# Row-run query tiles, fewer loads, accumulating dots and an event-listed end phase in a hard-max attention kernel

## The chip, the cores and the metric

The kernel runs on one core of one Trainium2 chip. The metric is the device time of one execution in microseconds (us), median over the runs.

## The reference

Four batches of 4096 queries and 4096 keys, 128 elements each, fp32. For each query the value row of the key with the largest dot product is wanted, nothing else.

```
def reference(q, k, v):                                   # each 4 x 4096 x 128, fp32
    logits = np.matmul(q, k.transpose(0, 2, 1))
    best = np.argmax(logits, axis=-1)
    b_idx = np.arange(q.shape[0])[:, None]
    return v[b_idx, best, :].astype(np.float32)
```

## The kernel before

The 128 query tiles (T = 128, 128 queries each) go through a pipeline of five engines, one tile per step of a loop that emits all engines' work in a fixed order:

- PE (TensorE) makes fp16 scores, folded so that one column stands for a group of four keys.
- ACT (ScalarE) evicts them: twice an absolute value (`A<-pd`) and once a relu (`E<-psn`).
- DVE (VectorE) takes the maximum over two halves (`W<-psn,E`, here "the fold") and then the eight largest (`TOP<-W`).
- POOL (GpSimd) gathers for each query the fp16 key differences of its best group (`kg`); DVE makes three dot products with the query (`D`) and picks the key, in chunks of 8 tiles; POOL gathers the value rows (`vr`); SP stores them.
- Near ties are found by `flag_segment` (twice: tiles 0-63, tiles 64-127) and solved again in fp32: gathers FR, FQ, three FK, exact dots, gather FV, scatter into the output.

POOL's work waits in three lists: `near_q` holds the key gathers, `fast` the gathers and the scatter of the re-check, `late_q` the value gathers and the stores. The *issue rule* says how many of each go out in one step.

The parts that the argument touches, with cuts marked:

```
def load_q(b, x, y):                     # a tile is 128 successive rows: runs of 512 bytes
    nc.gpsimd.dma_start(out=natq[b % 2][:, x:y], in_=q[b].rearrange("(t p) d -> p t d", p=P)[:, x:y])

def dots(c, x, m):                       # for m = 2 tiles
    yield "until", lambda: ("kg", x) in done, 2
    ...                                  # prod = kg * q;  p1, p2: two halving adds
    nc.vector.tensor_reduce(out=d[:, x - c0:x - c0 + m, 1:4], in_=p2, axis=AX_X, op=OP.add)

def issue(it):                           # once a step: what POOL is given
    if it > T + 1:
        while near_q:
            near_q.pop(0)()
        late = 2
    else:
        n = 0
        while near_q and (n < 1 or near_q[0] in marks):        # one key gather
            g = near_q.pop(0)
            n += g not in marks
            g()
        late = 2 if n == 0 and len(late_q) + len(fast) > 4 else 1   # and one value gather
    for _ in range(late):
        if fast or late_q:
            (late_q if late_q and it > T + 1 else fast or late_q).pop(0)()
        ...
```

Of the kernel before, what the change touches and what calls it, by code (L numbers as in the profile page):

```python
# [7 lines left out]
FP32 = mybir.dt.float32  # L8
# [13 lines left out]
TAU = 8.0  # L22
NEAR = 0.5


@with_exitstack
def kernel(ctx, tc, q, k, v, out):
# [24 lines left out]
    rec = dr.tile([P * T, 8], U32, name="rec")  # L52
    k16 = [dr.tile([NG, 384], FP16, name=f"k16_{b}") for b in range(B)]
# [5 lines left out]

    def load_k(b, h, x, y):  # L60
        kb = k[b].rearrange("(h p n) d -> p h n d", p=P, n=16)
        nc.gpsimd.dma_start(out=natk[b % 2][:, h, x:y], in_=kb[:, h, x:y])  # L62

    def load_q(b, x, y):
        nc.gpsimd.dma_start(out=natq[b % 2][:, x:y], in_=q[b].rearrange("(t p) d -> p t d", p=P)[:, x:y])  # L65
# [10 lines left out]
    def load_part(b, i):  # L76
        if b >= B:
            return
        if i < 8:
            load_k(b, i // 4, i % 4 * 4, i % 4 * 4 + 4)  # L80
        else:
            load_q(b, (i - 8) * NQT // 8, (i - 7) * NQT // 8)
# [18 lines left out]
    nc.vector.tensor_scalar(out=identn, in0=ident, scalar1=-1.0, scalar2=None, op0=OP.mult)  # L101
    for h in range(2):
        put_k(0, h)
    D_t = [cp.tile([P, 8, 4], FP32, name=f"D{i}", tag=f"D{i}") for i in range(3)]
# [23 lines left out]
    nc.gpsimd.tensor_scalar(out=tri, in0=iota_r, scalar1=iota_p, scalar2=1.0, op0=OP.subtract, op1=OP.is_gt)  # L128
    HARD = cp.tile([P, 1], FP32, tag="HARD")
# [100 lines left out]
    done, stores, marks = set(), set(), set()  # L230

    def gather(c, t0, n):
        c0, c1 = chunks[c]
        if t0 == c0:
            cand_t[c] = sp.tile([P, c1 - c0], U32, tag=f"cand{c1 - c0}", name=f"cand_{c}", bufs=3)
        x = cand_t[c][:, t0 - c0:t0 - c0 + n]
        nc.vector.tensor_scalar(out=x, in0=TOP.bitcast(U32)[:, t0:t0 + n, 0], scalar1=NG - 1, scalar2=NG - 1,
                                op0=OP.bitwise_and, op1=OP.bitwise_xor)
        kg = rp.tile([P, n, 3, P], FP16, tag=f"kg{n}", name=f"kg_{t0}", bufs=8)
        assert len(kg_t) < 8  # L240
        kg_t[t0] = kg
        for j in range(n):
            near_q.append(lambda j=j: nc.gpsimd.indirect_dma_start(  # L243
                out=kg[:, j].rearrange("p f d -> p (f d)"), out_offset=None, in_=k16[t0 // NQT],
                in_offset=IOA(ap=x[:, j:j + 1], axis=0)))
        mark = lambda: done.add(("kg", t0))
        marks.add(mark)
        near_q.append(mark)
        start(dots(c, t0, n), "dots")

    def dots(c, x, m):
        c0 = chunks[c][0]
        d = D_t[c % 3]
        b = x // NQT
        yield "until", lambda: ("kg", x) in done, 2
        kg = kg_t.pop(x)
        prod = rp.tile([P, m, 3, P], FP16, tag=f"prod{m}", name=f"prod_{x}")
        nc.vector.tensor_tensor(out=prod, in0=kg, in1=natq[b % 2][:, x - b * NQT:x - b * NQT + m, :].unsqueeze(2).to_broadcast([P, m, 3, P]),  # L258
                                op=OP.mult)
        yield "dve",  # L260
        p1 = rp.tile([P, m, 3, 64], FP16, tag=f"p1{m}", name=f"p1_{x}")
        nc.vector.tensor_tensor(out=p1, in0=prod[:, :, :, 0:64], in1=prod[:, :, :, 64:128], op=OP.add)  # L262
        yield "dve",
        p2 = rp.tile([P, m, 3, 32], FP16, tag=f"p2{m}", name=f"p2_{x}")
        nc.vector.tensor_tensor(out=p2, in0=p1[:, :, :, 0:32], in1=p1[:, :, :, 32:64], op=OP.add)  # L265
        yield "dve",
        nc.vector.tensor_reduce(out=d[:, x - c0:x - c0 + m, 1:4], in_=p2, axis=AX_X, op=OP.add)  # L267
        done.add(("dot", x))

    def pick(c, t0, t1):  # L270
        n = t1 - t0
        b, qt = t0 // NQT, t0 % NQT
        d = D_t[c % 3][:, 0:n, :]
        yield "until", lambda: all(("dot", x) in done for x in range(t0, t1, 2)), 0
# [3 lines left out]
        yield "dve",  # L278
        lt = sp.tile([P, n, 4], FP32, tag=f"lt{n}", name=f"lt_{c}")
        nc.vector.tensor_tensor(out=lt, in0=d, in1=mx.to_broadcast([P, n, 4]), op=OP.is_lt)  # L280
        yield "dve",
# [3 lines left out]
        yield "dve",  # L285
        wi = sp.tile([P, n], FP32, tag=f"wi{n}", name=f"wi_{c}")
        nc.vector.tensor_reduce(out=wi, in_=sel, axis=AX_X, op=OP.min)
        yield "dve",
        win = sp.tile([P, n], U32, tag=f"win{n}", name=f"win_{c}")
        nc.vector.scalar_tensor_tensor(out=win, in0=cand, scalar=4.0, in1=wi, op0=OP.mult, op1=OP.add)  # L290
        vr = rp.tile([P, n, P], FP32, tag=f"vr{n}", name=f"vr_{c}", bufs=3)
        for j in range(n):
            late_q.append(lambda j=j: nc.gpsimd.indirect_dma_start(out=vr[:, j, :], out_offset=None, in_=v_flat,  # L293
                                                                   in_offset=IOA(ap=win[:, j:j + 1], axis=0)))

        def store():
            nc.sync.dma_start(out=out[b, qt * P:(qt + n) * P, :].rearrange("(j p) d -> p j d", p=P), in_=vr)
            done.add(("out", c))

        stores.add(store)  # L300
        late_q.append(store)
        yield "dve",
# [3 lines left out]
        yield "dve",  # L306
        nc.vector.tensor_reduce(out=CNT[:, t0:t1], in_=near, axis=AX_X, op=OP.add)
        done.add(("cnt", c))

    def put_rec(t0, t1):  # L310
        nc.sync.dma_start(out=rec.rearrange("(p t) w -> p t w", t=T)[:, t0:t1, :], in_=TOP.bitcast(U32)[:, t0:t1, :])



    def flag_segment(t0, t1, ready, stored):
        yield "until", ready, 0
        S = t1 - t0
        H = fp.tile([P, S, 4], U32, tag="H", name=f"H_{t0}")
        nc.vector.tensor_scalar(out=H, in0=TOP.bitcast(U32)[:, t0:t1, 0:4], scalar1=16, scalar2=None,
                                op0=OP.logical_shift_right)  # L320
        yield "dve", 0.17
        F = fp.tile([P, S], FP32, tag="F", name=f"F_{t0}")
        nc.vector.scalar_tensor_tensor(out=F, in0=H[:, :, 1], scalar=TAU, in1=H[:, :, 0], op0=OP.add, op1=OP.is_ge)
        yield "dve", 0.17
        nc.vector.scalar_tensor_tensor(out=F, in0=CNT[:, t0:t1], scalar=1.5, in1=F, op0=OP.is_gt, op1=OP.max)
        yield "dve", 0.17
        F4 = fp.tile([P, S], FP32, tag="F4", name=f"F4_{t0}")
        nc.vector.scalar_tensor_tensor(out=F4, in0=H[:, :, 3], scalar=TAU, in1=H[:, :, 0], op0=OP.add, op1=OP.is_ge)
        yield "dve", 0.17
        Ec = fp.tile([P, S], FP32, tag="Ec", name=f"Ec_{t0}")  # L330
        nc.vector.tensor_tensor(out=Ec, in0=F, in1=codes[:, t0:t1], op=OP.mult)
        yield "dve", 0.17
        e8 = fp.tile([P, 8], FP32, tag="e8", name=f"e8_{t0}")
        nc.vector.max(out=e8, in_=Ec)
        yield "dve", 0.17
        val = fp.tile([P, 8], FP32, tag="val", name=f"val_{t0}")
        nc.vector.tensor_scalar(out=val, in0=e8, scalar1=0.5, scalar2=None, op0=OP.is_gt)
        yield "dve", 0.17
        n2 = fp.tile([P, 3], FP32, tag="n2", name=f"n2_{t0}")
        nc.vector.tensor_reduce(out=n2[:, 0:1], in_=val, axis=AX_X, op=OP.add)  # L340
        yield "dve", 0.17
        nc.vector.tensor_reduce(out=n2[:, 1:2], in_=F, axis=AX_X, op=OP.add)
        yield "dve", 0.17
        nc.vector.tensor_reduce(out=n2[:, 2:3], in_=F4, axis=AX_X, op=OP.add)
        yield "dve", 0.17
        yield "wait", 2
        ps = pp.tile([P, 1024], FP32, tag="u", name=f"fp_{t0}")
        nc.tensor.matmul(out=ps[:, 0:1], lhsT=tri, rhs=n2[:, 0:1], start=True, stop=True)  # L348
        nc.tensor.matmul(out=ps[:, 512:515], lhsT=ones, rhs=n2, start=True, stop=True)
        bs = fp.tile([P, 1], FP32, tag="bs", name=f"bs_{t0}")  # L350
        nc.vector.tensor_copy(out=bs, in_=ps[:, 0:1])
        yield "dve", 0.17
        tot = fp.tile([P, 3], FP32, tag="tot", name=f"tot_{t0}")
        nc.vector.tensor_copy(out=tot, in_=ps[:, 512:515])
        yield "dve", 0.17
        posn = fp.tile([P, 8], FP16, tag="posn", name=f"posn_{t0}")
        nc.vector.scalar_tensor_tensor(out=posn, in0=iota_r[:, 0:8], scalar=bs, in1=val, op0=OP.add, op1=OP.mult)
        yield "dve", 0.17
# [3 lines left out]
        yield "dve", 0.17  # L362
        rec2 = fp.tile([P, 8, 2], BF16, tag="rec2", name=f"rec2_{t0}")
        nc.vector.tensor_copy(out=rec2[:, :, 0], in_=e8)
        yield "dve", 0.17
        nc.vector.tensor_copy(out=rec2[:, :, 1], in_=iota_p.to_broadcast([P, 8]))
        yield "dve", 0.17
        yield "wait", 2
        ps2 = pp.tile([P, 1024], FP32, tag="u", name=f"fq_{t0}")
        for s in range(8):  # L370
            nc.tensor.matmul(out=ps2[:, 0:2], lhsT=OH[:, s, :], rhs=rec2[:, s, :], start=s == 0, stop=s == 7)
        tp = fp.tile([P, 2], FP32, tag="tp", name=f"tp_{t0}")
        nc.vector.tensor_copy(out=tp, in_=ps2[:, 0:2])
        yield "dve", 0.17
        rw = fp.tile([P, 2], FP32, tag="rw", name=f"rw_{t0}")
        nc.vector.tensor_scalar(out=rw[:, 0:1], in0=tp[:, 0:1], scalar1=0.5, scalar2=float(1 << 20), op0=OP.is_lt, op1=OP.mult)
        yield "dve", 0.17
        nc.vector.scalar_tensor_tensor(out=rw[:, 1:2], in0=tp[:, 0:1], scalar=float(P), in1=tp[:, 1:2], op0=OP.mult, op1=OP.add)
        yield "dve", 0.17
        row = fp.tile([P, 1], U32, tag="row", name=f"row_{t0}")  # L380
        nc.vector.scalar_tensor_tensor(out=row, in0=rw[:, 1:2], scalar=-float(P), in1=rw[:, 0:1], op0=OP.add, op1=OP.add)
        yield "dve", 0.17

        hd = fp.tile([P, 2], FP32, tag="hd", name=f"hd_{t0}")
        nc.vector.tensor_scalar(out=hd[:, 0:1], in0=tot[:, 1:2], scalar1=-float(P), scalar2=0.0, op0=OP.add, op1=OP.max)
        yield "dve", 0.17
        nc.vector.tensor_tensor(out=hd[:, 1:2], in0=tot[:, 1:2], in1=tot[:, 0:1], op=OP.subtract)
        yield "dve", 0.17
        for a in (hd[:, 0:1], hd[:, 1:2], tot[:, 2:3]):
            nc.vector.tensor_tensor(out=HARD, in0=HARD, in1=a, op=OP.add)  # L390
            yield "dve", 0.17

        rr = fp.tile([P, 1], U32, tag="rr", name=f"rr_{t0}")
        nc.vector.scalar_tensor_tensor(out=rr, in0=tp[:, 1:2], scalar=float(T), in1=tp[:, 0:1], op0=OP.mult, op1=OP.add)
        yield "dve", 0.17
# [20 lines left out]
        for r in range(3):  # L416
            get(FK[:, r, :], k4, gb[:, r:r + 1], B * NG)
# [215 lines left out]
```

## Time and profile before

| what | value | from |
|---|---|---|
| time | 502.46 us (501.86 to 503.29) | three runs |
| span | 498.3 us | the page; this execution took 500.26 us |
| first fold, last fold start | 20.8, 429.6 us | timeline of DVE |
| last fold to span end ("end phase") | 68.7 us | the same |
| per tile, tiles 20 to 75 | 3.15 us | fold start to fold start |

From the page, the busy time of each engine, and the busy tenths of DVE and ACT and the granted PE clock in 40 slices of the span:

```profile
PE 399.9 (80%) x1960; PEld 187.9 (38%) x1960; DVE 420.5 (84%) x833; ACT 394.5 (79%) x441; POOL 310.7 (62%) x345
...
DVE  2179999999999999999999899999999999972030
ACT  1999999999999999999989899999878999200000
...
PEclk9999999999999999999999999999999999755555
```

Two engines are full until the last fold. The windows say where each one binds (columns: stretch, its length, busy us of PE, PEld, DVE, ACT, POOL with instruction counts, granted clock, DMA share, GB/s): ACT in 75-100, where the next batch is transposed, and DVE in 200-250.

```profile
75.00:100.00 25.00, 23.13 (x125) 10.78 (x124) 23.80 (x41) 25.00 (x32) 15.23 (x16) 1.00 0.33 62
200.00:250.00 50.00, 47.20 (x212) 20.42 (x211) 50.00 (x91) 48.11 (x53) 34.84 (x39) 1.00 0.38 90
```

The waits of three groups (busy us, mean ns, then the engine's idle time just before them and what ended it). The closing re-check waits 20.0 us for its first gather, FR, which stands behind a backlog of value gathers on POOL:

```profile
L223 DVE TENSOR_TENSOR W<-psn,E 128x1024 int16<-128x1024 f32 x128 | 166.5, 1301 | 25.5 <-ACT E L210 16.4
L188 PEld LDWEIGHTS <-qT 128*128 128x128 f16 x1024 | 99.7, 99 | 159.3 <-issue 71.6
L411 DVE TENSOR_SCALAR gi<-FR 128x3 uint32<-128x3 uint32 x2 | 0.3, 157 | 20.0 <-DMA FR<-rec,rr 20.0
```

### The profile page before, as it was taken

The numbers are of one execution on the slowest core, as the hardware profiler recorded it, in microseconds if no ns is written. First come the engines' busy times: TensorE is split into PE (matmuls) and PEld (weight loads), VectorE is DVE, ScalarE is ACT, GpSimd is POOL, SyncE is SP. The second block draws the span as 40 slices with busy tenths as digits, with TensorE's granted clock in tenths as the row PEclk, the third lists the DMA queues.
The fourth block names the chain that finished last, engine by engine and source line by source line (L and its number), as shares of the span: only waits on it lengthen the run. The fifth ranks groups of instructions, "written<-read, shape, count | busy, mean of one in ns | idle before, by whom it ended". The sixth has DMA issues, their size and how long they took to land. (4 is left out here: it accounts for less than half of the span.)

```text
span 498.3 us, 6462 instructions
## 1 busy us (share of the span) xinstructions
PE 399.9 (80%) x1960; PEld 187.9 (38%) x1960; DVE 420.5 (84%) x833; ACT 394.5 (79%) x441; POOL 310.7 (62%) x345
## 2 busy tenths in 40 slices
PE   8999999999899999999999899989988999200000
PEld 5545554444345544443455444333333333100000
DVE  2179999999999999999999899999999999972030
ACT  1999999999999999999989899999878999200000
POOL 9124446566787886667888866566646666677730
PEclk9999999999999999999999999999999999755555
DMA  9714354132547672315456641323311313243410
GB/s 131 134 17 81 81 94 74 54 98 55 124 94 157 114 128 65 99 53 113 96 130 136 88 98 55 91 57 93 98 39 54 98 54 97 57 123 95 110 52 5
DMA packets 51751, 43.47 MB, mean 87 GB/s; under 512 B 24424, under 2 KB 45931, under 8 KB 51712
## 3 DMA queue, kind: packets, MB, share of 16 engines
q0 software_dynamic: 31520, 30.97, 31.3%
q1 hardware_dynamic: 20192, 12.06, 8.3%
q8 instruction: 15, 0.25, 0.2%
q14 instruction: 24, 0.20, 0.1%
HBM read 39.59 MB, written 12.19 MB: 104 GB/s over the span
## 5 line engine op out<-in xcount | busy, mean ns | idle before, releaser
L197 ACT ACTIVATE A<-pd 128x1024 f16<-128x1024 f32 x256 | 267.9, 1083 | 8.8 <-PE pd L188 8.4
L243 POOL DMA_INDIRECT kg<-k,cand x128 | 124.1, 970 | 123.3 <-DVE p L262 30.7
L223 DVE TENSOR_TENSOR W<-psn,E 128x1024 int16<-128x1024 f32 x128 | 166.5, 1301 | 25.5 <-ACT E L210 16.4
L188 PE MATMUL psn<-kT,qT 128*128 128x512 f16 x512 | 151.8, 377 | 19.5 <-ACT A L197 13.0
L188 PEld LDWEIGHTS <-qT 128*128 128x128 f16 x1024 | 99.7, 99 | 159.3 <-issue 71.6
L188 PE MATMUL pd<-kT,qT 128*128 128x512 f16 x512 | 152.4, 379 | 6.5 <-ACT A L197 6.2
L226 DVE MAX8 TOP<-W 128x8 f32<-128x1024 f32 x128 | 155.9, 1218 | 0.0
L207 PE MATMUL psn<-A,identh 128*128 128x512 f16 x512 | 152.0, 378 | 0.0
L293 POOL DMA_INDIRECT vr<-in_v_dram,win x128 | 126.9, 992 | 39.0 <-issue 36.9
L210 ACT ACTIVATE E<-psn 128x1024 int16<-128x1024 f32 x128 | 138.0, 1078 | 7.8 <-PE psn L207 7.1
L207 PEld LDWEIGHTS <-identh 128*128 128x128 f16 x512 | 49.5, 97 | 60.8
L258 DVE TENSOR_TENSOR prod<-kg,natq 128x768 f16<-128x768 f16 (+1 forms) x65 | 35.1, 541 | 2.9 <-DMA kg<-k,cand 2.9
L262 DVE TENSOR_TENSOR p<-prod 128x384 f16<-128x384 f16 (+1 forms) x65 | 22.3, 346 | 0.0
L65 POOL DMA_DIRECT2D natq<-in_q_dram x26 | 22.3, 858 | 0.1
L160 PE MATMUL uk<-identh,natk 128*128 128x128 f16 x96 | 22.2, 303 | 0.0
L267 DVE TENSOR_REDUCE D<-p 128x6 f32<-128x192 f16 (+1 forms) x65 | 21.6, 333 | 0.0
L163 ACT ACTIVATE kT<-uk 128x512 f16<-128x512 f32 x24 | 14.6, 606 | 4.2 <-PE uk L161 3.5
L170 ACT ACTIVATE qT<-uq 128x512 f16<-128x512 f32 x24 | 17.1, 710 | 0.9 <-PE uq L168 0.9
L411 DVE TENSOR_SCALAR gi<-FR 128x3 uint32<-128x3 uint32 x2 | 0.3, 157 | 20.0 <-DMA FR<-rec,rr 20.0
L348 PE MATMUL fp<-n,tri 128*128 128x1 f32 x4 | 0.9, 304 | 20.1 <-DVE n L340 20.1
L62 POOL DMA_DIRECT2D natk<-in_k_dram x26 | 15.7, 606 | 0.9 <-POOLq L617 0.8
L265 DVE TENSOR_TENSOR p<-p 128x192 f16<-128x192 f16 (+1 forms) x65 | 16.1, 250 | 0.0
(96 smaller groups left out, 205.3 us busy)
## 6 DMA issues: line engine op xcount, KB each, us to landing
out_dram<-vr SPq DMA_DIRECT2D x13, 512.0 KB, 3.4
k<-kd SPq DMA_DIRECT2D x8, 384.0 KB, 3.3
natk<-in_k_dram POOLq DMA_DIRECT2D x24, 128.0 KB, 4.0
natq<-in_q_dram POOLq DMA_DIRECT2D x24, 128.0 KB, 3.0
kg<-k,cand POOLq DMA_INDIRECT x128, 2.7
vr<-in_v_dram,win POOLq DMA_INDIRECT x128, 2.5
natk<-in_k_dram POOLq DMA_DIRECT2D x2, 512.0 KB, 5.4
out_dram<-vr SPq DMA_DIRECT2D x4, 256.0 KB, 2.3
```

Of the source, the lines that this page charges most:

```text
L65: nc.gpsimd.dma_start(out=natq[b % 2][:, x:y], in_=q[b].rearrange("(t p) d -> p t d", p=P)[:, x:y])
L160: nc.tensor.matmul(out=o, lhsT=natk[b % 2][:, h, 4 * m + x, :], rhs=identh, start=True, stop=False)
L188: nc.tensor.matmul(out=ps[:, n * 512:(n + 1) * 512], lhsT=qT[b % 2][:, qt * P:(qt + 1) * P], rhs=kT[b % 2][:, u * 1024 + n * 512:u * 1024 ...
L197: nc.scalar.activation(out=A, in_=ps, func=AF.Abs)
L207: nc.tensor.matmul(out=ps[:, n * 512:(n + 1) * 512], lhsT=identh, rhs=A[:, n * 512:(n + 1) * 512], start=False, stop=True)
L210: nc.scalar.activation(out=E, in_=ps, func=AF.Relu)
L223: nc.vector.tensor_tensor(out=W_t[t % NW].bitcast(I16)[:, 1::2], in0=ps, in1=E, op=OP.max)
L226: nc.vector.max(out=TOP[:, t, :], in_=W_t[t % NW].bitcast(FP32))
L243: near_q.append(lambda j=j: nc.gpsimd.indirect_dma_start(out=kg[:, j].rearrange("p f d -> p (f d)"), out_offset=None, in_=k16[t0 // NQT], ...
L258: nc.vector.tensor_tensor(out=prod, in0=kg, in1=natq[b % 2][:, x - b * NQT:x - b * NQT + m, :].unsqueeze(2).to_broadcast([P, m, 3, P]), op ...
L262: nc.vector.tensor_tensor(out=p1, in0=prod[:, :, :, 0:64], in1=prod[:, :, :, 64:128], op=OP.add)
L293: late_q.append(lambda j=j: nc.gpsimd.indirect_dma_start(out=vr[:, j, :], out_offset=None, in_=v_flat, in_offset=IOA(ap=win[:, j:j + 1], a ...
```

## The change

The intent: move queries and outputs in runs of 4 KB rather than 512 bytes, load each batch in 8 pieces rather than 16, replace the multiply-and-halve tree by accumulating dots, keep POOL fed so that no backlog of gathers is left at the end, and emit the last 36 tiles from a list of events with assumed durations, with the flagged rows' gathers ahead and the last two tiles solved directly in fp32. The core of the diff (flag arithmetic for the new rows, and the code of the event list, are cut):

```
+ND = 2
+TAIL = 36
+    def rows(x, b):
+        return x[b].rearrange("(p t) d -> p t d", t=NQT)
-        nc.gpsimd.dma_start(out=natq[b % 2][:, x:y], in_=q[b].rearrange("(t p) d -> p t d", p=P)[:, x:y])
+        nc.gpsimd.dma_start(out=natq[b % 2][:, x:y], in_=rows(q, b)[:, x:y])
-        if i < 8:
-            load_k(b, i // 4, i % 4 * 4, i % 4 * 4 + 4)
+        if i < 4:
+            load_k(b, i // 2, i % 2 * 8, i % 2 * 8 + 8)
 ...
+    def dot(acc, x, y, n, kind):
+        dump = rp.tile([P, P], x.dtype, tag=f"dump{kind}", name=f"dump_{n}", bufs=3)
+        nc.vector.tensor_tensor_reduce(out=dump, in0=x, in1=y, scale=1.0, scalar=0.0, op0=OP.mult, op1=OP.add, accum_out=acc)
 ...                                     # gather: one kg tile per query tile, 10 buffers
+        for f in range(3):
+            dot(D_t[c % 8][:, t - chunks[c][0], f + 1:f + 2], kg[:, f], natq[t // NQT % 2][:, t % NQT, :], f"{t}_{f}", "h")
 ...
+    def issue(spare):
+        if near_q:
+            send(near_q)
+        for _ in range(2 if spare and len(late_q) + len(fast) > 2 else 1):
+            if fast or late_q:
+                send(fast or late_q)
 ...
+    SEGS = [0, 48, E1]                   # E1 = T - ND
 ...
+    for it in range(T - TAIL):
 ...
+        step(it, False)                  # dots between fold and maximum
+        if it >= 2:
+            top(it - 2)
 ...
+        issue(qt >= 18 or qt % 2)        # in most steps: one key gather and up to two late ones
+    closing(T - TAIL - 1)                # the event list
+    nc.gpsimd.drain()
     man.__exit__(None, None, None)
     all_rows()
```

## The prediction

> **What bounds the kernel now.** Span 498.3 us. In the windowed table ACT is saturated while the next batch is transposed (25.0 of 25 us at 75-100), DVE elsewhere (50.0 of 50 at 200-250 and 350-400). By the fold starts in the timeline a tile takes about 3.24 us where ACT binds (some 48 tiles) and 3.02 us where DVE binds. Two stretches are worse: tiles 77-83 take 3.3-5.0 us (POOL issues a value gather, a key gather and a 0.82 us query load per tile, so query loads come late), 104-106 take 4.1-4.5 us (six 0.6 us steps of the first flag segment). First fold at 20.8, last at 429.6. Then comes the 68.7 us end phase: DVE finishes picks and flags by 452, but POOL works off a backlog of value gathers, 1.25 us each, until 469.5; only then the re-check's gathers (DVE waits 20.0 us for FR in the waits view), three key gathers, six DVE steps of 0.7 us, value gather, scatter (ends 485.8). The last 12.5 us are program end, 7.7 of them a POOL drain from 489.7.
>
> **What the change does.**
> 1. End phase: no backlog, the re-check's gathers first, two last tiles solved directly in fp32. Estimate from trace durations, from last fold start X: last max ends X+2.6; six direct key gathers until X+7.8; one-hot X+9; FR issued X+12, lands X+15; three FK gathers until X+19.5; last dots X+23; scatter done X+27.5. Before: X+56. Gain 28 us.
> 2. The added POOL drain starts right after the scatter instead of 4 us later: 2-4 us saved if its length stays.
> 3. Dots. Before, per tile, start to start: half of 0.49+0.27+0.17+0.25 = 0.59 us. After: three tensor_tensor_reduce; the order listing shows each followed by a second instruction writing 128x1. [...]
> 4. Loads in 4 KB runs, 8 per batch instead of 16: the stall at tiles 77-83 goes, -6 us. The re-check's dots spread better: -1.
>
> ACT and PE work per tile is unchanged.
>
> **Sum.** Last fold about 431; scatter done 458.5; span 468.5; timed 471 (timed minus profiled span was 4.2; I take 2.5-4). Eight in ten within 461-482. Faster by over 2%: 0.95; within 2%: 0.03; slower: 0.02.
>
> **What would show it.** Last fold to span end 36-40 us instead of 69; no run of value gathers on POOL after DVE's last pick; FR's wait under 5 us;[...] fold spacing 3.05-3.25 where DVE binds; no fold gap above 4 us near tiles 77-83; drain within 1 us of the scatter.
>
> **What would make it wrong.** A dot above 0.3 us puts DVE above ACT everywhere: +15 us or more.[...] The drain's length, if it depends on what is outstanding, moves 4 us. If real costs differ from those the event order assumes, in-order engines wait for late gathers in the last 36 tiles.

The sum came to 431 us for the last fold, 468.5 for the span and 471 timed, and one of its terms is cut. The last fold of before, 429.6, less 6 for the loads and 1 for the re-check's dots, is 422.6; the other 8 us or so up to 431 are the cost of the accumulating dots, which the author had estimated without a trace behind it. The 0.3 us that would put DVE above ACT stays: as an estimate from the trace's 3.02, 0.59 and 3.24, 3.02 - 0.59 + 3 x 0.3 is 3.33 us a tile, over ACT's 3.24.

## More of the kernel before

The profiled execution is not one of the timed ones, and neither it nor they name a chip.

The view of DMA issues (last number: median us from issue to landing) will matter later only because its last number is there:

```profile
kg<-k,cand POOLq DMA_INDIRECT x128, 2.7
vr<-in_v_dram,win POOLq DMA_INDIRECT x128, 2.5
```

## The result, and the profile after

| | before | after |
|---|---|---|
| time, median of 4 runs | 502.53 us (501.86 to 503.29) | 548.07 us (542.40 to 549.61) |
| profiled span | 498.3 us | 546.7 us |
| last fold start | 429.6 us | 505.7 us |
| end phase | 68.7 us | 40.9 us |

The ratio is 1.0885 (95%: 1.0806 to 1.0964): slower by 9%, where 6% faster was predicted. Ratios are the mean time of one kernel's fast runs over that of the other's of the same rounds, so not quite the ratio of the medians quoted. All four runs of after are labelled fast, but that label compares executions of one kernel with each other, and all four are alike. The record of this result doesn't name its chip.

The same lines of the page as before. DVE and ACT are no longer full, and the PE clock dips again and again:

```profile
PE 423.1 (77%) x1962; PEld 192.9 (35%) x1962; DVE 438.4 (80%) x1433; ACT 398.2 (73%) x441; POOL 290.7 (53%) x325
...
DVE  3279995894999895897959798696999899979840
ACT  1999995984988895976859697784779798766000
...
PEclk9999998896999997897979999897999999989555
```

In the same windows, DVE has fallen from 50.00 to 40.97 busy us of 50 in 200-250, ACT from 25.00 to 18.88 of 25 in 75-100, and the clock below 0.9:

```profile
75.00:100.00 25.00, 18.57 (x90) 8.11 (x89) 17.35 (x53) 18.88 (x23) 13.34 (x14) 0.86 0.22 68
200.00:250.00 50.00, 40.09 (x175) 16.79 (x174) 40.97 (x127) 36.93 (x44) 24.80 (x26) 0.89 0.18 54
```

The waits: the fold's idle time has nearly tripled, PE's idle time before weight loads has risen by 57 us, most of it put down to "issue", that is to nothing that the profile shows, and the re-check no longer waits for FR:

```profile
L234 DVE TENSOR_TENSOR W<-psn,E 128x1024 int16<-128x1024 f32 x128 | 166.7, 1302 | 72.2 <-ACT E L221 38.7
L199 PEld LDWEIGHTS <-qT 128*128 128x128 f16 x1024 | 102.1, 101 | 216.3 <-issue 135.8
L411 DVE SCALAR_TENSOR_TENSOR gb<-FR,bo 128x3 uint32<-128x3 uint32 x2 | 0.3, 170 | 0.7 <-DMA FR<-rec,row 0.7
```

So the end phase came out nearly as intended and the main loop lost 76 us. It did not lose them evenly. The fold starts show a normal pace broken by stalls: 9.0 us between two folds at tile 21, 8.8 at 30, 9.0 at 53, 8.7 at 69, 8.0 at 85, 12.5 at 91, with smaller ones after most of them. Here is the first, on PE, ACT and DVE (start, duration, engine, line, operation, count, and in brackets the idle time before it and its releaser):

```profile
86.25 0.39 PE L179 MATMUL uq<-identh,natq 128*128 128x128 f16 x4
...
87.34 0.59 PE L199 MATMUL psn<-kT,qT 128*128 128x512 f16 x2 [0.27 <-issue]
87.77 0.59 PE L218 MATMUL psn<-A,identh 128*128 128x512 f16 x2
...
91.38 0.38 PE L179 MATMUL uq<-identh,natq 128*128 128x128 f16 x4 [0.88 <-ACT A L208]
95.56 1.01 PE L199 MATMUL pd<-kT,qT 128*128 128x512 f16 x2 [3.79 <-ACT E L221]
...
88.83 0.60 ACT L181 ACTIVATE qT<-uq 128x512 f16<-128x512 f32 x1 [1.55 <-PE pd L199]
90.31 1.02 ACT L208 ACTIVATE A<-pd 128x1024 f16<-128x1024 f32 x1 [0.88 <-PE pd L199]
94.48 1.02 ACT L221 ACTIVATE E<-psn 128x1024 int16<-128x1024 f32 x1 [3.15 <-remote]
...
95.54 1.30 DVE L234 TENSOR_TENSOR W<-psn,E 128x1024 int16<-128x1024 f32 x1 [5.96 <-ACT E L221]
```

PE is done with `uq` at 86.64, but ACT, free since 87.3, starts `qT<-uq` only at 88.83. PE is done with this tile's first `psn` at 88.36, but ACT, free since 91.33, starts `E<-psn` only at 94.48: six us after the work, three of them idle. PE meanwhile has run out of free accumulators and waits for ACT, 3.79 us; DVE waits for ACT too, 5.96 us. The work was done and its release came late. The trace's records of semaphore updates, which no view prints, show it. PE's semaphore counts up at the end of each group of matmuls (in the trace of before all 591 updates but the two of the program's end are stamped within 0.02 us of one); the six groups from `uq` on end at 86.64, 87.07, 88.36, 88.79, 90.51 and 91.77, and the six updates recorded after that of the group before them are stamped 88.81, 90.23 and, while PE idles, 94.46, 94.50, 94.56 and 94.62. ACT's three instructions above start 0.02, 0.08 and 0.02 us after the first three stamps. (As records are missing in this trace, the pairing rests on the equal number and on these starts; the releasers in brackets, a `pd` for `qT<-uq`, are the tool's guess.) ACT's own update for `A<-pd` is stamped 91.34, 0.01 us after its end. When PE's release comes, PE's granted clock is 0.50, and the next matmul pair takes 1.01 us instead of 0.59. (The records of the clock give 0.50 from 92.3 to 99.1. The half-clock stretches in the loop last 3.4, 6.8 or 10.2 us. What sets them off is not shown: this one begins 0.5 us into the idle 3.79, and in the 3.4 us before it PE was busy for 1.4.)

One more thing is different in this trace: the DMA view lacks its last column.

```profile
kg<-k,cand POOLq DMA_INDIRECT x126
vr<-in_v_dram,win POOLq DMA_INDIRECT x126
```

The landing times are gone because about half of the records of semaphore updates are missing: the trace of before holds 8,025 of them, this one 4,069. The instruction records are complete (the same counts as in a later trace of the same kernel). As the trace of before may be of another chip, this difference need not be one of the two kernels.

### The profile page after: what moved, and what is told of

It reads as the page before. It is cut to its first block, busy times and chain, and to the rows that moved or that the text cites. A ratio compares the mean times of both kernels' runs of the same rounds, so it can differ in the third digit from the quotient of the medians.

```text
span 546.7 us, 7066 instructions
## 1 busy us (share of the span) xinstructions
PE 423.1 (77%) x1962; PEld 192.9 (35%) x1962; DVE 438.4 (80%) x1433; ACT 398.2 (73%) x441; POOL 290.7 (53%) x325
## 5 line engine op out<-in xcount | busy, mean ns | idle before, releaser
L199 PE MATMUL psn<-kT,qT 128*128 128x512 f16 x512 | 158.4, 392 | 42.2 <-ACT A L208 14.2
L199 PE MATMUL pd<-kT,qT 128*128 128x512 f16 x512 | 158.3, 392 | 30.6 <-issue 14.9
L218 PE MATMUL psn<-A,identh 128*128 128x512 f16 x512 | 158.4, 392 | 0.0
L262 POOL DMA_INDIRECT vr<-in_v_dram,win x126 | 121.4, 963 | 43.1 <-issue 38.1
L269 DVE CUSTOM_DVE_ANT_0 dump<-kg,natq 128x128 f16<-128x128 f16 x378 | 89.4, 286 | 3.7 <-DVE D L269 1.9
L269 DVE DVE_READ_ACCUMULATOR2_ANT D<- 128x1 f32 x378 | 31.3, 83 | 0.0
L171 PE MATMUL uk<-identh,natk 128*128 128x128 f16 x96 | 22.2, 303 | 1.6 <-ACT E L221 1.6
L172 PEld LDWEIGHTS <-natk 128*128 128x128 f16 x96 | 12.3, 128 | 5.3 <-issue 3.7
L276 DVE TENSOR_SCALAR cand<-TOP 128x2 uint32<-128x2 uint32 (+1 forms) x82 | 13.1, 160 | 0.6
L171 PEld LDWEIGHTS <-natk 128*128 128x128 f16 x96 | 12.3, 129 | 2.8
L172 PE MATMUL uk<-identh,natk 128*128 128x128 f16 x48 | 11.6, 314 | 0.0
L172 PE MATMUL uk<-identn,natk 128*128 128x128 f16 x48 | 11.6, 314 | 0.0
```

The lines of the kernel that those rows point to most:

```text
L171: nc.tensor.matmul(out=o, lhsT=natk[b % 2][:, h, 4 * m + x, :], rhs=identh, start=True, stop=False)
L172: nc.tensor.matmul(out=o, lhsT=natk[b % 2][:, h, 4 * m + x + 1, :], rhs=identn if u % 2 else identh, start=False, stop=True)
L199: nc.tensor.matmul(out=ps[:, n * 512:(n + 1) * 512], lhsT=qT[b % 2][:, qt * P:(qt + 1) * P], rhs=kT[b % 2][:, u * 1024 + n * 512:u * 1024 ...
L218: nc.tensor.matmul(out=ps[:, n * 512:(n + 1) * 512], lhsT=identh, rhs=A[:, n * 512:(n + 1) * 512], start=False, stop=True)
L262: return queue(q, lambda: nc.gpsimd.indirect_dma_start(out=dst, out_offset=None, in_=src, in_offset=IOA(ap=idx, axis=0), **kw), after)
L269: nc.vector.tensor_tensor_reduce(out=dump, in0=x, in1=y, scale=1.0, scalar=0.0, op0=OP.mult, op1=OP.add, accum_out=acc)
```

## The experiments

The table gathers all runs; the texts follow in the order in which they were made. "Last fold" is its start, "end phase" the rest of the span, "stalls" the fold gaps over 7 us before tile 91 (where the event list takes over in the changed kernel), and "longest" the most gathers (key and value) that POOL issued in that part of the loop with less than 1.45 us from start to start, that is with neither a pause nor a load between them. Runs with one execution have state unknown and no interval.

| run | chip | us | before | last fold | end phase | stalls | longest |
|---|---|---|---|---|---|---|---|
| (result) before | not named | 502.53 | | 429.6 | 68.7 | 0 | 6 |
| (result) after | not named | 548.07 | 502.53 | 505.7 | 40.9 | 5 | 12 |
| e1_before_ttr | 13 | 512.41 | 503.66 | 436.5 | 73.9 | 0 | 6 |
| e2_after_tree | 13 | 577.98 | 503.66 | 534.0 | 42.2 | 3 | 10 |
| e3_after_16loads | 13 | 534.71 | 503.66 | 494.9 | 38.0 | 4 | 12 |
| e5_after_six_plain | 13 | 589.97 | 503.66 | 547.4 | 40.8 | 0 (five of 5.7 to 6.8) | 10 |
| b1_before_rows | 4 | 501.84 | 500.69 | 429.5 | 70.5 | 0 | 5 |
| b2_after_norows | 4 | 488.34 | 500.69 | 446.8 | 39.7 | 0 | 12 |
| b3_after_gentle | 4 | 497.98 | 500.69 | 444.9 | 51.3 | 0 | 4 |
| b4_before_issue | 4 | 486.69 | 500.69 | 430.4 | 54.5 | 0 | 11 |
| c1_after_again (4 runs) | 1 | 488.60 | 500.16 | 446.2 | 40.5 | 0 | 12 |
| v1_best (4 runs) | 1 | 488.77 | 500.16 | 445.4 | 41.5 | 0 | 12 |
| v2_before_queues (4 runs) | 14 | 483.99 | 499.90 | 430.1 | 51.9 | 0 | 11 |
| x1_before_rows_issue | 14 | 486.82 | 499.90 | 429.6 | 55.4 | 0 | 10 |
| x2_after_gentle_norows | 14 | 497.09 | 499.90 | 444.6 | 50.8 | 0 | 4 |
| x3_after_landing | 14 | 485.94 | 499.90 | 443.9 | 40.3 | 0 | 12 |
| v3_before_queues (4 runs) | 13 | 565.51 | 503.66 | 508.0 | 54.9 | 6 | 11 |
| c2_after_third | 13 | 552.10 | 503.66 | 509.4 | 40.9 | 7 | 12 |
| v4_every_fourth (4 runs) | 11 | 487.28 | 500.05 | 428.5 | 57.4 | 0 | 9 |
| x6_after_gentle_landing | 11 | 499.99 | 500.05 | 444.9 | 53.3 | 0 | 4 |

### First theories: the dots, the loads (chip 13)

The first theory was that the accumulating dots hold DVE up; rivals were the many small DVE instructions and the larger load pieces. One kernel adds the dots alone to before:

```
-        (prod, p1, p2, tensor_reduce)
+            nc.vector.tensor_tensor_reduce(out=dump, in0=kg[:, j, f], in1=natq[...], ..., accum_out=d[:, ..., f + 1:f + 2])
```

> The kernel before, with only its candidate dots replaced by tensor_tensor_reduce (six per pair of tiles). Theory A, the accumulator pairs stall the other engines: fold gaps of 8 to 12 us appear in the main loop as in the changed kernel, half of the semaphore-release records go missing (many waits read 'issue' or 'remote'), last fold near 480 instead of 429.6, time about 545 us. Theory B, the stalls come from the row layout or the loads: no fold gap over 6 us, last fold 428 to 440, time 500 to 512 us.

It took 512.41 us, its last fold is 7 us later than that in the trace of before (which may be of another chip), and it has no gap over 7 us. Three more kernels undo one part each of the changed kernel: the dots as the old tree, one tile at a time; the loads in 16 pieces; the dots as three multiplications and three reductions.

```
 e2: -  three tensor_tensor_reduce        + prod, p1, p2, tensor_reduce over one tile
 e3: -  load_k(b, i // 2, ...), i < 4     + load_k(b, i // 4, ...), i < 8, loads at the steps of before
 e5: -  three tensor_tensor_reduce        + three times tensor_tensor, tensor_reduce
```

> The changed kernel, with only its candidate dots put back to one multiply, two halvings and one reduce per tile[...]. Theory A: the long gaps go, last fold 430 to 445, end phase as in the changed kernel (about 41 us from last fold to span end), time 472 to 492 us. Theory B: the gaps of 8 to 12 us stay, time 545 us or more.

> The changed kernel with the loads of the next batch put back into 16 pieces at the old tiles. Theory A: the gaps stay, time 540 to 556 us. Theory B in its form with the loads: gaps fall to those of before, time 475 to 490 us.

> The changed kernel with each tensor_tensor_reduce replaced by a plain multiply and a plain reduce: still six small DVE instructions per tile with six results, no accumulator. Theory A (the accumulator instructions themselves): no gaps over 6 us,[...] fold spacing about 3.4 us, last fold about 455, time 495 to 510 us. Theory C (the number of small DVE instructions and their semaphores): gaps of 8 to 12 us remain and time is 560 us or more.

(In e2's trace the four steps take 1.07 us, from 330.24 to 331.31.)

They took 577.98, 534.71 and 589.97 us, and all stall at nearly the same tiles (30 and 53 or 54 in each). For e5 neither forecast fits: over 560 us, but no gap over 6.8 before tile 91. So neither the dots nor the loads alone are needed for the stalls. All four traces miss some 40% of the semaphore records (4,517 to 4,881 are left), e1 without a gap over 7 us: lost records do not by themselves bring stalls of that size.

### Halving the rest (chip 4)

What remained were the row layout, the issue rule and the loop order. Four kernels take them one by one from either side:

```
 b1 (before): q, out by rows(); row = p * 32 + (t & 31) + (t >> 5) * 4096
 b2 (after):  rows() is "(t p) d -> p t d" again, flag arithmetic likewise
 b3 (after):  - issue(qt >= 18 or qt % 2)                         + issue(False)
 b4 (before): - late = 2 if n == 0 and len(late_q) + len(fast) > 4 else 1
              + late = 2 if (it % NQT >= 18 or it % 2) and len(late_q) + len(fast) > 2 else 1
```

> The kernel before with nothing but the row-run layout of the query tiles (queries and outputs move as 4 KB runs, eight tiles of a chunk at a time). If the layout is what makes PE's releases late, stalls over 4.2 us appear in the main loop and the time goes to 525 to 550 us. If the layout is innocent, the main loop keeps its pace (last fold at 428 to 433 us, as before's 429.6) and the time stays within 500 to 505 us.

> The changed kernel with the old tile layout (512-byte rows). If the layout is the cause, the stalls go: last fold near 440 us and time near 480 us. If it is innocent, time stays at 535 to 560 us with stalls at the same tiles (21, 30, 53, 62, 85, 91).

> The changed kernel with at most one gather of the value rows issued per tile step, never two (the end phase untouched). If POOL's back-to-back gathers are the cause of the late PE releases, the stalls go and the time falls to 475 to 490 us. If they are innocent, the time stays at 535 to 560 us with stalls at the same tiles.

> The kernel before with the changed kernel's issue rule alone (one near gather plus up to two late ones in most steps). If back-to-back gathers are the cause, stalls over 4.2 us appear at chunk intervals and the last fold moves from 429.6 to 450 to 500 us. If they are innocent, the last fold stays within 427 to 433 us, and the end phase may even be shorter, as the value gathers are done earlier (495 to 503 us).

Taken at face value, undoing either the layout (488.34 us) or the issue rule (497.98) cures the changed kernel, while neither harms before (501.84; and with the issue rule 486.69, faster than before by 14.0 us). That would mean that only both together stall. But these runs were made on another chip, and their traces were complete. A control was due before believing in an interaction.

### The control: the changed kernel, unchanged, on another chip

> The changed kernel itself once more, as a control: the earlier experiments ran on one chip and the last four on another. If the row layout and the issue rule together cause the stalls whatever the chip, the time is 540 to 552 us again with the stalls of 8 to 12 us at tiles 21, 30, 53, 91. If the stalls belong to the chip, the time is about 486 to 500 us, with no gap over 7 us before tile 91, as in the two runs of the changed kernel on this last chip.

It took 488.60 us over four runs, before 500.16 in the same rounds; ratio 0.9771 (0.9755 to 0.9788). The same program that was 9% slower is here 2.3% faster. The cures of b2 and b3 were no cures: there was nothing to cure on that chip.

The two traces run the same instructions on every engine, and until 88.8 us no PE, ACT or DVE instruction starts later by more than half a microsecond in one than in the other. The first to do so is the `qT<-uq` that opens the stall shown above. In the control the same stretch is this, PE and then ACT:

```profile
85.77 0.39 PE L179 MATMUL uq<-identh,natq 128*128 128x128 f16 x4
...
86.85 0.59 PE L199 MATMUL psn<-kT,qT 128*128 128x512 f16 x2 [0.27 <-ACT A L208]
87.28 0.59 PE L218 MATMUL psn<-A,identh 128*128 128x512 f16 x2
...
86.50 0.79 ACT L181 ACTIVATE qT<-uq 128x512 f16<-128x512 f32 x1
86.97 1.23 ACT L208 ACTIVATE A<-pd 128x1024 f16<-128x1024 f32 x1
87.91 1.21 ACT L221 ACTIVATE E<-psn 128x1024 int16<-128x1024 f32 x1
```

ACT does not idle. `E<-psn` starts at 87.91, within 0.05 us of the end of its matmuls (87.87); it is the one that started at 94.48 in the result's trace. The whole control looks like before: its PE clock stays up, and the landing times are back.

```profile
DVE  3179999999999999999999999989999999999830
ACT  1999999999998999988899999988888888870000
...
PEclk9999999999999999999999999999999999996555
```

```profile
kg<-k,cand POOLq DMA_INDIRECT x126, 2.7
vr<-in_v_dram,win POOLq DMA_INDIRECT x126, 2.5
```

In the control no `A<-pd` starts more than 0.4 us after both its matmuls have ended and ACT is free; in the result's trace 12 of 256 do, by up to 6.0 us. The update records say the same for every run. Call one of PE's late if it is stamped over 0.1 us after the end of the last matmul that carries one. In the result's trace 64 of 481 are late (the two of the program's end left out), in the control and the twelve other complete traces none; ACT has no late one in any trace. So the stalls are late releases by PE, and whether they happen depends on the chip, or on something that goes with it, such as its host.

A first combined version: tile layout, paired tree dots, always up to two late gathers, the event list with landing times set.

```
 v1 (b2): + pair(c, x): prod, p1, p2, tensor_reduce for two tiles; issue(True)
          + in closing: the last three key gathers land 2.5, 4.0, 5.5 us after its start
```

> A combined version: tile layout and paired tree dots of the kernel before, issue rule always up to two late gathers, end phase of the changed kernel with landing times set at its start. If the parts add up: last fold at 430 to 436 us, 40 us of end phase, 470 to 478 us, free of stalls. If the stalls follow from the issue rule alone after all, over 500 us.

It took 488.77 us, no better than the changed kernel: its last fold came at 445.4 instead of 430 to 436. The loss is in the tiles of the event list, as in the changed kernel (below).

### What is left on a chip without stalls (chip 14)

> The kernel before with up to two late gathers a step, near gathers first and the flagged rows' gathers ahead of the last four value gathers at the end, flagged-row dots by accumulation, and the drain before the closing branch. If the gain of the change lies in the order of POOL's queue and the end phase, and not in the event list: last fold at 429 to 432 us, end phase 42 to 48 us, time 473 to 481 us on a chip without stalls. If the event list is needed for the end phase, 485 us or more.

> The kernel before with row layout and the changed kernel's issue rule together. On a chip without stalls: 485 to 489 us, as with the issue rule alone (486.7). On a chip that stalls the changed kernel: if layout and issue rule are the trigger, over 510 us with gaps of 8 us and more; if the trigger is elsewhere, 487 to 492 us.

> The changed kernel with neither row layout nor double late gathers. On a chip without stalls: 494 to 500 us, as with the gentle rule alone (498.0). On a chip that stalls the changed kernel: if layout or issue rule is the trigger, the same 495 to 503 us; if the loop order and the single-tile gathers are, over 530 us.

> The changed kernel with the event list told that the last three gathers before its start have yet to land. On a chip without stalls: if the 9.1 us gap at tile 91 is a wrong landing time in the list, the gap shrinks to under 5 us and the time to 482 to 485 us; if the gap has another cause, 487 to 490 us. On a chip that stalls the changed kernel: 535 us or more.

```
 v2 (before): late = 2 if len(late_q) + len(fast) > 2 else 1
              after the last tile: key gathers first; FR, FQ ahead of the last four value gathers
              exact(): 12 tensor_tensor_reduce in place of 3 x (tensor_tensor, tensor_reduce)
              nc.gpsimd.drain() before the closing branch
 x1 (b1):     the issue rule of b4
 x2 (b2):     issue(False)
 x3 (after):  in closing: the last three key gathers land 2.5, 4.0, 5.5 us after its start
```

The chip has no stalls. x1 shows that layout and issue rule together are harmless here (486.82 us, with the rule alone 486.69). x2 shows the price of the gentle rule (never two late gathers in a step), 497.09. x3, at 485.94 between its two forecasts, gains a little: the fold gap at tile 91 falls from 9.1 to 5.5 us, though the next two tiles give some of it back (4.4 at 93). v2 is the fastest kernel: 483.99 us against 499.90, ratio 0.9677 (0.9661 to 0.9693). It missed the 473 to 481 us expected: its end phase, 51.9 us, stayed longer than the 42 to 48 expected, because the last pair's keys still waited behind four value gathers (a 3.71 us wait of DVE) and POOL then idled 3.1 us before the re-check's first gather.

### Back to chip 13, by chance

v3 was to remove that wait: no value gathers in the last four steps, and the double issue only where the changed kernel has it. Before its last steps it differs from before in the issue rule alone, apart from the flagged rows' dots of the first segment, which come long after the first stalls.

```
 v3 (v2): - for _ in range(2 if len(late_q) + len(fast) > 2 else 1):
          + for _ in range(0 if it > T - 4 else 2 if (it % NQT >= 18 or it % 2) and len(late_q) + len(fast) > 2 else 1):
```

> v2_before_queues with no value gathers issued in the last steps, so that the last key-group gathers are not behind them, and the double issue held back in the load steps as in the changed kernel. If POOL's order is what held the last dots: the 3.7 us DVE wait for the last pair's keys falls under 2 us and the time is 479 to 483 us where before takes 500; if the wait only moves to the flagged rows' gathers behind the value gathers, 483 to 486 us. On a chip that stalls the changed kernel, 480 to 487 us if the loop of before is immune, over 505 us if the issue rule is the trigger.

> The changed kernel itself again, for the chip: 487 to 490 us with no gap over 7 us before tile 91 on a chip without stalls, 540 to 552 us on one with them.

Both stall: c2, the changed kernel itself, took 552.10 us, with its stalls at tiles 21, 30, 53, 62, 69, 75 and 85, the result's five among them. That ties the result to this kind of chip. And v3, with the loop, the layout and the dots of before, took 565.51 us, ratio 1.1228 (1.113 to 1.1326). Its first stall begins at about 93 us; POOL, PE and ACT around it:

```profile
93.17 0.94 POOL L293 DMA_INDIRECT vr<-in_v_dram,win  x1 [0.30 <-issue]
94.42 0.94 POOL L293 DMA_INDIRECT vr<-in_v_dram,win  x1 [0.31 <-issue]
95.67 0.95 POOL L243 DMA_INDIRECT kg<-k,cand  x1 [0.30 <-issue]
96.92 0.95 POOL L243 DMA_INDIRECT kg<-k,cand  x1 [0.30 <-issue]
...
92.02 0.39 PE L168 MATMUL uq<-identh,natq 128*128 128x128 f16 x4
...
94.75 0.60 ACT L170 ACTIVATE qT<-uq 128x512 f16<-128x512 f32 x1 [1.70 <-PE pd L188]
```

PE's `uq` ends at 92.4, ACT gets to it at 94.75. The four gathers are the last of eleven without a pause, from 84.1 to 96.9. Compare e1 on the same chip, whose loop never has more than six in a row. It has no gap over 7 us, but at its run of six, and nowhere else in the loop at this size, the same thing happens on a smaller scale: `uq` ends at 192.16, its update is stamped 194.85, and ACT idles 2.19 us.

```profile
194.88 0.60 ACT L170 ACTIVATE qT<-uq 128x512 f16<-128x512 f32 x1 [2.19 <-PE psn L207]
```

Of e1's PE updates 5 of 456 are late, of v3's 69 of 489. In one window, e1 first, then v3 (columns as above):

```profile
110.00:135.00 25.00, 23.65 (x105) 9.90 (x104) 25.00 (x79) 24.40 (x27) 16.40 (x18) 1.00 0.35 82
```

```profile
110.00:135.00 25.00, 17.71 (x64) 6.77 (x63) 16.80 (x30) 15.20 (x17) 13.75 (x14) 0.77 0.25 67
```

So on chip 13 the issue rule is enough to bring stalls of this size, without row layout, accumulating dots, larger loads, single-tile gathers or event list. And v2, whose rule is if anything denser (eleven in a row too), ran on chip 14 without one. Both are needed for them: the denser issue rule, and such a chip. What in the rule does it is not shown. Every run of ten or more gathers in the result's loop goes with late PE updates, but of 13 bursts of them there (over 0.5 us late) six come at runs of at most five. Nor do other counts separate the kernels that stall from those that do not, or the denser rule from the old: with loads counted too, e1 issues up to 32 DMAs without a pause and v3 19, and the densest 10 us before tile 91 hold 207 recorded DMA increments in the trace of before and 208 in the control.

### The last call

Two kernels with a thinner rule were to show on chip 13 whether that removes the stalls:

```
 v4 (v3): - 2 if (it % NQT >= 18 or it % 2) and len(late_q) + len(fast) > 2 else 1
          + 2 if (n == 0 or it % 4 == 3) and len(late_q) + len(fast) > 4 else 1
 x6 (x3): - issue(qt >= 18 or qt % 2)      + issue(False)
```

> v3_before_queues with a second value gather only in every fourth step and only when more than four wait. On a chip without stalls: last fold 429 to 432 us, some value gathers left over for the end phase, 482 to 490 us. On chip 13: if stalls need runs of 8 or more back-to-back gathers, and this rule makes few of them in the main loop, under 500 us; if any added gather is too much there, over 520 us.

> The changed kernel with never more than one value gather a step in the main loop, and the event list's landing times set. On a chip without stalls: 493 to 498 us, as b3_after_gentle less the gap at tile 91. On chip 13: if back-to-back gathers are the trigger, no gap over 7 us before tile 91 (later ones may remain, as the end phase still sends gathers back to back) and under 515 us; if another part of the changed loop is the trigger, the gaps at tiles 21, 30, 53, 69, 85 stay and the time is over 530 us.

The call fell on chip 11, which has no stalls, so the question stays open. v4 took 487.28 us (ratio 0.9746, 0.973 to 0.9762), within what was expected. x6 took 499.99 us, above the 493 to 498 expected: the landing times, worth 2 us with the denser rule, gave nothing here.

### What is shown and what is open

Shown: the result's 548 us are a property of the kernel and the chip together (that the result's unnamed chip is of the stalling kind is inferred from c2's like stalls). On the one chip known to stall, the changed kernel took 552.1 us; over four runs on another it took 488.6. Before hardly notices such a chip: 503.66 us on chip 13, 499.9 to 500.7 on the others. The stalls are PE releases that arrive up to 6.6 us after the work (in the result's trace). On chip 13 all five kernels with the changed issue rule stall (e5 with gaps of at most 6.8 us), and the one with the old rule (e1) has only the short one shown. The seven traces with lost records, the result's and those of chip 13, are the seven with late PE updates.

Not shown: why the denser gathers go with late releases of PE there. The complete traces give how many updates a DMA makes: the control's 350 DMAs stand beside 5,575 recorded updates of theirs, of 7,814 in all, and in the trace of before 368 DMAs beside 5,865 of 8,025, some 16 each. A gather every 1.25 us then makes, as an estimate from these numbers, 13 updates per us. On chip 13 some 40 to 48% of the update records are lost, and ACT's updates come late in no trace: whatever holds up PE's does not hold up every engine's. Whether the recording has a part in it no run here can tell, since there was none without records. Also open: whether the changed kernel with the gentle rule is free of stalls on chip 13, and how common such chips are. Of the five chips met one stalls; the result's own may be the same one.

## Why the prediction was wrong

The prediction was 471 us, the result 548.07. Two different errors are in it, and the runs on other chips separate them.

1. **End phase, "Gain 28 us": right.** 40.9 us in the result and 40.5 on chip 1, just above the predicted 36-40, before 68.7. FR's wait fell from 20.0 to 0.7 us, predicted under 5. b4 shows that about half of this (68.7 to 54.5) comes from the issue rule alone, which leaves no backlog.
2. **The drain, "2-4 us saved if its length stays": half right.** From the scatter's issue to the end of the span, 13.5 us became 12.1 (in the result and on chip 1): 1.4 us saved. The drain starts with the scatter, as predicted, but its length did not stay: 8.70 us instead of 7.75. The new place is not shown to be the reason: b1 and x1, whose drain still comes 4 us after the scatter, have 9.06, and e3, with it at the scatter, 2.94.
3. **Dots, the cut term, some 8 us: right in size, in part by luck.** A dot follows the last after 0.21 us. Tiles 20 to 75 took 3.25 us on chip 1 against 3.15 before; in e1, on chip 13, 3.23. But from start to start the dots' own share of a tile there rose only from 0.60 to 0.645 us; 0.07 more came from the flagged rows' work, which the change moved into this stretch, and DVE idled 0.04 less. What the author had put down for one dot was an estimate without a trace behind it; the profile's 0.21 decides, in which the read of the accumulator adds nothing to the time between two dots:

```profile
202.43 0.28 DVE L269 CUSTOM_DVE_ANT_0 dump<-kg,natq 128x128 f16<-128x128 f16 x1
202.63 0.09 DVE L269 DVE_READ_ACCUMULATOR2_ANT D<- 128x1 f32 x1
202.63 0.29 DVE L269 CUSTOM_DVE_ANT_0 dump<-kg,natq 128x128 f16<-128x128 f16 x1
```

   (These are two dots of the result's timeline; the read of one accumulator starts with the next dot.)

4. **Loads, "the stall at tiles 77-83 goes": right on a chip without stalls.** The 5.0 us gap at tile 82 of before is absent from the control; b4 and x1, with 16 loads, still have one of 5.1 and 5.4 there. (v2, with 16 loads and a denser rule, has 3.8: the loads are not the only cure.) Tiles 77 to 83 together take 3.7 us less than before, of the 6 predicted. With points 3 and 4 together, fold 90 of the control starts at 314.6 against 313.1.
5. **The sum, "Last fold about 431": this step failed, twice.** On chip 1 the last fold starts at 446.2, 15 us late. Between folds 90 and 91, at the switch to the event list, 9.1 us pass instead of some 3: DVE makes twelve more dots than in a usual step and a second maximum, and waits 1.9 us for the keys of one tile, which have not landed (no later instruction goes ahead of them: the next fold, whose `E` was done by 316.74, starts at 323.76).

```profile
321.67 0.29 DVE L269 CUSTOM_DVE_ANT_0 dump<-kg,natq 128x128 f16<-128x128 f16 x1 [1.92 <-DMA kg<-k,cand]
```

   The remaining 36 tiles take 3.40 us each instead of 3.15: 9 us more, and not by waiting. In the window of the control DVE is busy for 120.58 of 122 us, and waits for keys once, for 0.2 us:

```profile
324.00:446.00 122.00, 97.67 (x404) 38.88 (x402) 120.58 (x399) 95.38 (x100) 78.12 (x82) 0.99 0.30 83
```

   From start to start, DVE spends per tile 0.10 us more than before on dots, in line with the cut term, 0.11 more on picks, 0.04 on candidates, 0.08 on fold and maximum, and 0.09 less on flagged rows. The prediction had named "late gathers in the last 36 tiles" as a risk and put no number on it; waits for them cost 2 us. What its sum left out is more DVE work, at the switch and in these tiles. That is why even the undisturbed changed kernel takes 488.6 us, outside the range of 461-482.
6. On the result's chip the last fold starts at 505.7, another 60 us late. The premise that failed is "**ACT and PE work per tile is unchanged**": the work is, but it was taken to follow that its releases come on time. The 0.95 for "faster" rested on a trace of before, whose POOL never issues more than six gathers in a row in the loop. That trace, complete and with no late update, could not show what a denser rule does, nor that it depends on the chip.

The half of the end phase's gain that came cheapest was not seen as a part by itself: before with nothing but the denser issue rule (b4, 486.69 us) is as fast, on a chip without stalls, as the whole change.

## What to carry to other kernels

Before bisecting a loss that looks like nothing the change did, run the very same kernel on another chip: here two kernels seemed to cure, and two not to cause, a fault that their chip did not have. If the program is the same, compare two traces instruction by instruction; what the first late one waits for is the release that was late. A rule that keeps a DMA-issuing engine busier may be part of a gain of 13 to 16 us on some chips (4, 11 and 14 here: b4, v4, v2) and of a loss of 62 on another (13: v3), so time it on several before keeping it: v2 (483.99 us) beats both kernels on chip 14, and its near relative v3 takes 565.51 on chip 13.
